# Conditioning sums spread over more stages of a two-layer diffusion step, and eight weight splits moved to VectorE

## The chip, the cores and the metric

The kernel runs on one core of a Trainium2 chip. The metric is the device time of one execution in microseconds (us), as the median of several runs. The engines are TensorE (PE in the profile, PEld its weight loads), VectorE (DVE), ScalarE (ACT), GpSimd (POOL) and SyncE (SP), whose queue issues most of the DMAs.

## The reference

One inference step of a network with two layers, in fp32. 1024 latent tokens and 128 context tokens, each 1024 wide, go through both layers. Layer 0 mixes tokens with a recurrent block, layer 1 with latent attention; each is followed by an MLP with a squared ReLU. Every sub-layer is normalized and then shifted, scaled and gated by vectors that come from a conditioning vector:

```python
def adaln_params(cond, w_ada, b_ada):
    mod = jax.nn.silu(cond) @ w_ada + b_ada
    return jnp.split(mod, 6, axis=-1)

def sq_relu_mlp(h, w1, w2):
    a = jax.nn.relu(h @ w1)
    return (a * a) @ w2

# per layer l, for the context (cond = c_ctx) and for the latents (cond = c):
sh1, sc1, g1, sh2, sc2, g2 = adaln_params(cond, ada_w[l], ada_b[l])
h = modulate(rms_norm(x, norm_mix[l]), sh1, sc1)
...   # recurrent block or attention, its projection first
x = x + g1[:, None, :] * out
h = modulate(rms_norm(x, norm_mlp[l]), sh2, sc2)
x = x + g2[:, None, :] * sq_relu_mlp(h, mlp_w1[l], mlp_w2[l])
```

## The kernel before

All activations stand transposed (features on the partitions) in three chunks of 384 tokens. Each matrix product is made of three fp32r matmuls (`mm3`, lines 145, 148 and 149): both operands are split into a high part and a rest, `hi` by a cast on ACT (line 163) and `lo` by a subtraction (line 164) on the engine that the caller names, VectorE or GpSimd. Weights stream through SBUF as pieces of 128 x 1024: a piece is loaded into one of two buffers `raw` (line 111), split into a pair `whi`, `wlo` of a small rotating set (`wslot`), and used. A `raw` buffer is free when its split is done.

The order of the work is written out by the program, engine by engine; a scheduler of the framework then moves instructions on each queue by its own estimate of the times, except where `keep_in_program_order` holds them.

**Conditioning sums.** Of the twelve vectors of both layers, seven (56 groups of 128 features) are computed with dot products: `ada` loads 128 rows of the transposed `ada_w` into a buffer (`raw` too, or one of its own in the second matrix; line 178) and `ada_dot` multiplies them on VectorE by the condition and accumulates, once for each of two conditions (line 169; the first half writes to `junk`, the second over the rows). I call a load and its two halves a sum. The 56 sums are a list that is taken off in order. Eight are taken in layer 0's output projection; 24 in the 16 passes over its first MLP matrix (one and two in turn); 24 in the second matrix, one whenever a weight buffer of the kind `g` is taken. Layer 1's MLP runs the same code with the list empty.

**The MLP** (`mlp`, called for both layers). The first matrix is multiplied in 16 passes, each with products of sums and differences of the operands (a scheme that needs seven products for eight). A pass takes two weight rows: `prep` loads them and splits them in three parts, `R0` and `R1` (on GpSimd in layer 0, on VectorE in layer 1) and, after four subtractions of raw weights on VectorE (line 454, `raw<-raw`), `TY` and `TX` on VectorE. Results are stored to DRAM as nine hidden tiles for each of eight groups (line 417 and its kin; four of a pass from SP). For the remaining rows there are four groups of plain products (`filler`), two ahead of the passes and two behind. While the last two run, the hidden tiles (`hid`, line 563) and the residual (`X`, line 579) are loaded back for the second matrix. That runs in 16 steps: GpSimd makes the differences of weights (line 599) and splits them, VectorE splits the hidden tiles and adds the results to the residual with the gate (line 334).

**Behind the MLP of layer 0** comes the attention's projection (`mla`): per chunk, VectorE computes the factor of the norm (`rstd`, lines 267 to 281), PE spreads it over partitions (line 288), VectorE and ACT write the normalized chunk (lines 315 and 320), and PE multiplies it with the weights of the first four output groups, then of three more.

Of the kernel before, what the change touches and what calls it, by code (L numbers as in the profile page):

```python
# [50 lines left out]
RG_STREAM = list(dict.fromkeys((_k, _n // 2 * 2 if _k == "g" else _n) for _k, _n, *_ in RG_ORDER))  # L51
# [14 lines left out]
class Emit:  # L66
    def __init__(self, nc, tc, ins, outs):
        self.nc, self.tc, self.I, self.O = nc, tc, ins, outs
        self.piece_i = 0
        self.opened = []  # L70
        self.pending = []
        self.wpx = None
        self.pin = False
        self.cap = 1 << 30
        self.upx = self.gx = None
        self.wcycle, self.wi = ["wp"], 0
        self.ready = []
        self.used, self.oldest = set(), 0
        self.ada_i = 0
        self.ada_jobs = []  # L80
        self.ada_quota = 0.0
        self.ada_rate = 0.0
# [12 lines left out]
    def prefetch(self, upto):  # L95
        nc = self.nc
        if self.wpx is None:
            upto = min(upto, len(RG_STREAM) + 3)
        while self.piece_i < min(upto, self.cap, len(STREAM)):
            raw = self.raw(STREAM[self.piece_i])  # L100
            eng = nc.vector if self.piece_i < len(RG_STREAM) else nc.gpsimd
            self.ready.append(self.wsplit(raw, eng))
            self.piece_i += 1
            self.ada_quota += self.ada_rate
            n = int(self.ada_quota)
            self.ada_quota -= n
            self.ada(n)
# [6 lines left out]
    def wslot(self):  # L114

        kind = self.wcycle[self.wi % len(self.wcycle)]
        self.wi += 1
        if kind == "g":
            self.ada(1, self.gx)
        pool, n = {"wp": (self.wp, 3), "x": (self.wpx, 1), "u": (self.upx, 1), "g": (self.gx, 4)}[kind]  # L120
        return tuple(pool.tile([128, 1024], F32R, tag=t, name=t, bufs=n) for t in ("whi", "wlo"))

# [48 lines left out]
                op0=ALU.mult, op1=ALU.mult, accum_out=self.mod[:, l, j, cond, k:k + 1],  # L171
            )

    def ada(self, n, room=None):
        for l, j, k in self.ada_jobs[:n]:
            w = (room or self.wp).tile([128, 1024], F32, tag="ada" if room else "raw", name="raw", bufs=1 if room else 2)
            n0 = (j * 8 + k) * 128
            self.nc.sync.dma_start(w, self.I["ada_wt"][l, n0:n0 + 128])
            self.ada_dot(w, l, j, k, 0, 1)
            if k == 7:  # L180
                self.mod_finish(l, j)
        del self.ada_jobs[:n]
# [226 lines left out]
    def mlp(self, p0, base, l, H, after_acc, after):  # L409
        nc = self.nc  # L410
# [26 lines left out]
        def filler(i0, n, f=None):  # L437
            if f:
                bring2.append(f)
            for i in range(i0, i0 + n, 4):  # L440
                self.group([(plain[i + j], p0 + i + j, range(8)) for j in range(4)], rhs, drain2, chunks=[2])
# [15 lines left out]
        def prep(p, part):  # L457
            if p == 16:
                if part:
                    self.cap = p0 + 8 + part  # L460
                    self.prefetch(self.cap)
                return
            m = 4 * (p // 2) + p % 2
            if part == 0:
                r = [self.raw(up_row(i), *((self.upx, 4) if p else ())) for i in (m, m + 2)]
                W[p] = {"r": r, "R0": self.wsplit(r[0], leng)}
                return
            w = W[p]
            r0, r1 = w["r"]
            a, b = slice(0, 512), slice(512, 1024)  # L470
            if part == 1:
                w["R1"] = self.wsplit(r1[:, b], leng, 512)
                add(r0[:, a], r1[:, a], r0[:, a], ALU.subtract)
                add(r1[:, a], r1[:, b], r1[:, a], ALU.subtract)
                add(r1[:, b], r1[:, b], r0[:, a], ALU.subtract)
                add(r0[:, b], r0[:, b], r1[:, b], ALU.subtract)
            else:
                w["TY"] = self.wsplit(r1, nc.vector)
                w["TX"] = self.wsplit(r0, nc.vector)

        self.wcycle, self.wi = ["wp", "wp", "wp", "x", "u"], 0
        for i in range(3):
            prep(0, i)
        tail = None
        for p in range(16):
            m = 4 * (p // 2) + p % 2
            w = W.pop(p)
# [55 lines left out]
                add(e, h12, d, ALU.subtract)  # L543
                put(m, 7, e, nc.sync)

            self.ada(1 + p % 2)
        tail()
        self.cap = p0 + 16
        self.release(self.upx)
# [31 lines left out]
            load((2, 4, 5, 6, 7, 8, 9, 9)[i], True)  # L581

        filler(8, 8, bring)
        load(12)

        self.release(self.gpool)
# [23 lines left out]
        for d in range(16):  # L610
# [3 lines left out]
            for i in range(2):  # L614
                n = 2 * d + i
                m = 2 * (n % 4)
# [451 lines left out]
    def mla(self):  # L1068
        nc, tc, I, O = self.nc, self.tc, self.I, self.O
# [7 lines left out]
        def drain(m, c, ps):  # L1077
            nc.scalar.copy(out=raw[c][:, m], in_=ps)
            if m < 4:
                self.sq_acc(stq[c], raw[c][:, m], m)  # L1080
            elif m < 6:
                self.sq_acc(stk[c], raw[c][:, m], m)

        def rq(c):
            yield 2.9
# [41 lines left out]

        rhs = lambda k, c: (H[c][0][:, k], H[c][1][:, k])
        self.dense(pi, range(4), rhs, drain, rq)
        self.release(self.xp, self.cbp)  # L1130
        keep = self.alloc(name="keep", bufs=1, side="right", reuse_waits="tile")
        ckv = [keep.tile([128, 2, NK], F32R, name=f"ckv{i}") for i in range(2)]
# [431 lines left out]
```

## Time and profile before

| | |
|---|---|
| median of 3 runs | 2857.14 us (2857.11 to 2859.36) |
| the profiled execution | 2860.27 us, span 2858.2 us, mean granted clock of TensorE 0.973 |
| first MLP matrix of layer 0, 16 passes | from 534 to 843 us of the span |
| second MLP matrix of layer 0 | from 896 to 1319 us |
| attention's projection, first half | from 1326 us |
| first MLP matrix of layer 1, 16 passes | from 2104 to 2398 us |
| second MLP matrix of layer 1 | from 2447 to 2836 us |

A row of the profile names the line, the engine, the operation and the tiles (`out<-in`), then how often, and its busy time and mean duration; idle time stands with what ended it, as in `[5.02 <-POOL wlo L164]`: idle for 5.02 us until GpSimd's instruction of line 164 on `wlo` was done. A stretch `A:B` is in us from the span's start.

### The profile page before, as it was taken

To read this page: it belongs to the slowest core of one execution; us is meant where nothing else is said; L and a number is where in the kernel's file an instruction comes from. 1 tells how busy PE (TensorE), PEld (TensorE's weight loads), DVE (VectorE), ACT (ScalarE), POOL (GpSimd) and SP (SyncE) were. 2 spreads that over 40 slices of the span, in tenths; PEclk is the share of its full clock that TensorE was granted. 3 is DMA by queue.
4 is the path that set the end of the run, shared out by engine and by line. 5 is a ranking of instruction groups with operands and counts; after the bars stand their busy time and mean duration, and the time that the engine had idled before them with its cause. 6 is when DMAs were issued, how large, how long until landed. Compare 5 with 4: busy or idle time off the path is not lost.

```text
span 2858.2 us, 40872 instructions
## 1 busy us (share of the span) xinstructions
PE 2663.3 (93%) x15355; PEld 2566.0 (90%) x15355; DVE 1945.2 (68%) x3445; ACT 1384.3 (48%) x2446; POOL 893.0 (31%) x560
## 2 busy tenths in 40 slices
PE   5999999999997989998997999998999999899997
PEld 2878899999996878998997999998999999799997
DVE  6788877896545999677465767762675554477777
ACT  4577834545443223334324878871465555333332
POOL 1000023212225877773242000001300002777774
PEclk9999999999998999999998999999999999999998
DMA  6122244474446444334135111116344345433332
GB/s 253 45 81 83 87 156 142 162 229 162 144 130 247 159 145 162 111 111 140 52 110 166 62 47 52 48 52 208 116 151 142 130 145 188 149 122 118 122 123 106
DMA packets 145718, 368.67 MB, mean 129 GB/s; under 512 B 15472, under 2 KB 77744, under 8 KB 143088
## 3 DMA queue, kind: packets, MB, share of 16 engines
q1 hardware_dynamic: 121712, 331.44, 34.6%
q10 hardware_dynamic: 23040, 31.47, 3.1%
q0 software_dynamic: 768, 3.15, 0.4%
q8 instruction: 121, 1.98, 0.3%
q14 instruction: 77, 0.63, 0.1%
HBM read 268.83 MB, written 94.54 MB: 127 GB/s over the span
## 4 chain that ended last, share of the span: by engine, by line
PE 41%; DVE 5%; DMA 3%; POOL 2%; issue 2%; ACT 2%; SPq 0%; DVEq 0%; ACTq 0%; POOLq 0%
PE ps L145 9%; PE ps L148 9%; PE ps L149 9%; PE ps L1317 2%; DMA raw<-wts 2%; POOL wlo L164 1%; PE ps L1261 1%; PE ps L1264 1%; PE ps L1265 1%; PE ps L1262 1%; PE ps L1263 1%; PE ps L1343 1%; PE ps L1342 1%; PE ps L1341 1%; POOL raw L599 1%
## 5 line engine op out<-in xcount | busy, mean ns | idle before, releaser
L164 POOL TENSOR_TENSOR wlo<-raw,whi 128x1024 fp32r<-128x1024 f32 x233 | 569.8, 2453 | 1662.5 <-ACT whi L163 1399.2
L163 ACT CAST whi<-raw 128x1024 fp32r<-128x1024 f32 (+1 forms) x349 | 347.6, 1008 | 671.7 <-POOL raw L599 269.1
L145 PE MATMUL ps<-hhi,whi 128*128 128x384 f32 x1576 | 533.0, 342 | 22.0 <-ACT hhi L319 10.3
L148 PE MATMUL ps<-hlo,whi 128*128 128x384 f32 x1576 | 536.4, 340 | 13.7 <-DVE hlo L320 13.4
L149 PE MATMUL ps<-hhi,wlo 128*128 128x384 f32 x1576 | 532.6, 340 | 8.2 <-POOL wlo L164 7.9
L145 PE MATMUL ps<-hid,whi 128*128 128x384 f32 x1408 | 480.0, 344 | 51.3 <-DVE X L334 33.5
L334 DVE SCALAR_TENSOR_TENSOR X<-ps,mod,X 128x384 f32<-128x384 f32 (+2 forms) x768 | 379.4, 534 | 204.8 <-PE ps L149 171.0
L148 PE MATMUL ps<-hid,whi 128*128 128x384 f32 x1408 | 477.8, 339 | 0.0
L149 PE MATMUL ps<-hid,wlo 128*128 128x384 f32 x1408 | 462.9, 339 | 2.5 <-POOL wlo L164 2.5
L145 PEld LDWEIGHTS ps<-hid,whi 128*128 128x128 f32 x1408 | 269.0, 191 | 67.1 <-DVE X L334 39.1
L145 PEld LDWEIGHTS ps<-hhi,whi 128*128 128x128 f32 x1576 | 300.3, 191 | 32.2 <-ACT hhi L319 11.5
L148 PEld LDWEIGHTS ps<-hlo,whi 128*128 128x128 f32 x1576 | 300.9, 191 | 17.1 <-DVE hlo L320 17.0
L149 PEld LDWEIGHTS ps<-hhi,wlo 128*128 128x128 f32 x1576 | 300.6, 191 | 11.7 <-POOL wlo L164 10.0
L164 DVE TENSOR_TENSOR hid<-hid 128x768 fp32r<-128x768 f32 x144 | 208.1, 1465 | 92.5 <-ACT hid L163 92.5
L149 PEld LDWEIGHTS ps<-hid,wlo 128*128 128x128 f32 x1408 | 267.1, 190 | 3.3 <-POOL wlo L164 3.3
L148 PEld LDWEIGHTS ps<-hid,whi 128*128 128x128 f32 x1408 | 269.8, 192 | 0.0
L599 POOL TENSOR_TENSOR raw<-raw 128x256 f32<-128x256 f32 x256 | 252.8, 990 | 17.9
L164 DVE TENSOR_TENSOR wlo<-raw,whi 128x1024 fp32r<-128x1024 f32 x116 | 136.4, 1186 | 128.3 <-ACT whi L163 127.5
L163 ACT CAST hid<-hid 128x768 fp32r<-128x768 f32 x144 | 117.4, 834 | 157.4 <-DMA hid<-hid 143.8
L1266 DVE TENSOR_REDUCE mx<-ps 128x1 f32<-128x384 f32 (+1 forms) x200 | 108.6, 543 | 76.5 <-PE ps L1265 75.0
L148 PE MATMUL ps<-S,whi 128*128 128x384 f32 x384 | 130.4, 340 | 6.1 <-DVE S L164 6.1
L149 PE MATMUL ps<-S,wlo 128*128 128x384 f32 x384 | 130.4, 340 | 1.6 <-DVE wlo L164 1.5
(213 smaller groups left out, 5194.5 us busy)
## 6 DMA issues: line engine op xcount, KB each, us to landing
raw<-wts SPq DMA_DIRECT2D x221, 512.0 KB, 3.8
hid<-hid SPq DMA_DIRECT2D x144, 384.0 KB, 4.7
raw<-ada_wt SPq DMA_DIRECT2D x56, 512.0 KB, 3.8
hid<-st ACTq DMA_DIRECT2D x128, 192.0 KB, 2.0
hid<-st SPq DMA_DIRECT2D x128, 192.0 KB, 1.9
adaw<-ada_n SPq DMA_DIRECT2D x24, 512.0 KB, 4.3
xs<-X SPq DMA_DIRECT2D x6, 1536.0 KB, 5.4
X<-xs SPq DMA_DIRECT2D x12, 768.0 KB, 9.5
```

What stands on the lines that cost most here:

```text
L145: mm = nc.tensor.matmul(ps, lhsT=w[0], rhs=h[0], start=first, stop=False, **kw)
L148: nc.tensor.matmul(ps, lhsT=w[0], rhs=h[1], start=False, stop=False, **kw)
L149: nc.tensor.matmul(ps, lhsT=w[1], rhs=h[0], start=False, stop=last, **kw)
L163: nc.scalar.copy(out=hi, in_=src)
L164: (lo_eng or nc.vector).tensor_tensor(out=lo, in0=src, in1=hi.bitcast(F32), op=ALU.subtract)
L334: self.nc.vector.scalar_tensor_tensor(out=self.X[c][:, m, a:b], in0=ps[:, a:b], scalar=self.mod[:, l, j, cond, m:m + 1], in1=self.X[c][:, ...
L599: sub = lambda out, x, y: nc.gpsimd.tensor_tensor(out=out, in0=x, in1=y, op=ALU.subtract)
L1261: nc.tensor.matmul(ps, lhsT=qh, rhs=kh[:, a:b], start=True, stop=False)
L1262: nc.tensor.matmul(ps, lhsT=qh, rhs=kl[:, a:b], start=False, stop=False)
L1263: nc.tensor.matmul(ps, lhsT=ql, rhs=kh[:, a:b], start=False, stop=False)
L1266: nc.vector.tensor_reduce(out=mx[:, j:j + 1], in_=ps, axis=AX.X, op=ALU.max)
L1317: nc.tensor.transpose(ps[:, j * 128:(j + 1) * 128], p[:, (t * 3 + j) * 128:(t * 3 + j + 1) * 128], self.ident)
```

## The change

Three things. (1) In the first matrix two sums are taken in each pass from the third on (28 for 24), with their loads held in program order. (2) In the second matrix only every third buffer of the kind `g` takes a sum (12 for 24), and the last eight are taken in the attention's projection, at the drains of three of its first four groups. (3) From the last pass over the first matrix to the end of the plain groups behind it, the pieces of weights (eight in each layer) are split by VectorE and not by GpSimd.

```diff
@@ class Emit: __init__, prefetch
+        self.on_dve = False
...
-            eng = nc.vector if self.piece_i < len(RG_STREAM) else nc.gpsimd
+            eng = nc.vector if self.piece_i < len(RG_STREAM) or self.on_dve else nc.gpsimd
             self.ready.append(self.wsplit(raw, eng))
@@ wslot
         if kind == "g":
-            self.ada(1, self.gx)
+            if self.ada_i % 3 == 0:
+                self.ada(1, self.gx)
+            self.ada_i += 1
@@ ada
-    def ada(self, n, room=None):
+    def ada(self, n, room=None, pin=False):
...
-            self.nc.sync.dma_start(w, self.I["ada_wt"][l, n0:n0 + 128])
+            ld = self.nc.sync.dma_start(w, self.I["ada_wt"][l, n0:n0 + 128])
+            if pin:
+                self.tc.keep_in_program_order(ld)
@@ mlp: prep
             if p == 16:
                 if part:
+                    self.on_dve = True
                     self.cap = p0 + 8 + part
                     self.prefetch(self.cap)
@@ mlp: the loop over 16 passes, and behind it
-            self.ada(1 + p % 2)
+            if p > 1:
+                self.ada(2, pin=True)
...
         filler(8, 8, bring)
+        self.on_dve = False
         load(12)
@@ mla: drain, and behind the first four groups
+            if 0 < m < 4:
+                self.ada(1)
...
         self.dense(pi, range(4), rhs, drain, rq)
+        self.ada(len(self.ada_jobs))
         self.release(self.xp, self.cbp)
```

Lines of the new kernel stand a few numbers further on (169 becomes 172, 454 becomes 459, 178 becomes 181).

First place: VectorE in a steady pass over layer 0's first matrix. `st` are results of the pass, `raw` the weights that are subtracted, `wlo` the splits that the next pass needs. Before:

```order
L454 TENSOR_TENSOR st<-st 128x384 x3
L454 TENSOR_TENSOR raw<-raw 128x512
L454 TENSOR_TENSOR st<-st 128x384
L454 TENSOR_TENSOR st<-ps,cell 128x384
L454 TENSOR_TENSOR raw<-raw 128x512 x2
L454 TENSOR_TENSOR st<-ps,cell 128x384
L454 TENSOR_TENSOR raw<-raw 128x512
L454 TENSOR_TENSOR st<-ps,cell 128x384
L164 TENSOR_TENSOR wlo<-raw,whi 128x1024 x2
```

The same place in the new kernel:

```order
L459 TENSOR_TENSOR st<-st 128x384
L459 TENSOR_TENSOR st<-ps,cell 128x384
L459 TENSOR_TENSOR raw<-raw 128x512
L172 SCALAR_TENSOR_TENSOR junk,mod<-raw,cb 128x1024
L172 SCALAR_TENSOR_TENSOR raw,mod<-raw,cb 128x1024
L172 SCALAR_TENSOR_TENSOR junk,mod<-raw,cb 128x1024
L172 SCALAR_TENSOR_TENSOR raw,mod<-raw,cb 128x1024
L459 TENSOR_TENSOR raw<-raw 128x512
L459 TENSOR_TENSOR st<-ps,cell 128x384
L459 TENSOR_TENSOR raw<-raw 128x512
L459 TENSOR_TENSOR st<-ps,cell 128x384
L167 TENSOR_TENSOR wlo<-raw,whi 128x1024 x2
```

The four halves of two sums now stand between the second and the third subtraction of raw weights.

Second place: SP's queue in layer 0's second matrix. `hid_2` to `hid_4` are the hidden groups that are loaded ahead, `wts` weights, `ada_wt` the rows of a sum. Before:

```order
L111 DMA raw<-wts 128x1024
L178 DMA raw<-ada_wt 128x1024
L563 DMA hid<-hid_2 128x768 x3
L563 DMA hid<-hid_3 128x768 x3
L111 DMA raw<-wts 128x1024
L178 DMA raw<-ada_wt 128x1024
L111 DMA raw<-wts 128x1024
L178 DMA raw<-ada_wt 128x1024 x2
L111 DMA raw<-wts 128x1024
L563 DMA hid<-hid_3 128x768 x2
```

In the new kernel, from the twelfth sum's load on:

```order
L181 DMA raw<-ada_wt 128x1024
L570 DMA hid<-hid_2 128x768 x2
L112 DMA raw<-wts 128x1024
L570 DMA hid<-hid_2 128x768 x2
L112 DMA raw<-wts 128x1024
L570 DMA hid<-hid_2 128x768 x3
L570 DMA hid<-hid_3 128x768 x3
L112 DMA raw<-wts 128x1024 x3
L570 DMA hid<-hid_3 128x768 x2
```

All twelve loads stand ahead of the first row of this piece or in it; behind it the queue holds hidden tiles and weights alone.

Third place: VectorE where layer 0's MLP ends and the attention's projection begins. `X<-ps` are the last residuals of the third chunk, `cell` and `hlo` the first chunk's normalization, `sv` opens the second chunk's factor. Before:

```order
L252 TENSOR_TENSOR acc<-acc,cell 128x384
L334 SCALAR_TENSOR_TENSOR X<-ps,mod,X 128x256
L334 SCALAR_TENSOR_TENSOR X<-ps,mod,X 128x128
L315 SCALAR_TENSOR_TENSOR cell<-X,mod,ps 128x384
L320 SCALAR_TENSOR_TENSOR hlo<-cell,mod,hhi 128x384
L315 SCALAR_TENSOR_TENSOR cell<-X,mod,ps 128x384
L267 TENSOR_SCALAR sv<-ps 128x3
```

The same place in the new kernel:

```order
L172 SCALAR_TENSOR_TENSOR raw,mod<-raw,cb 128x1024
L257 TENSOR_TENSOR acc<-acc,cell 128x384
L339 SCALAR_TENSOR_TENSOR X<-ps,mod,X 128x256
L339 SCALAR_TENSOR_TENSOR X<-ps,mod,X 128x128
L320 SCALAR_TENSOR_TENSOR cell<-X,mod,ps 128x384
L172 SCALAR_TENSOR_TENSOR junk,mod<-raw,cb 128x1024
L325 SCALAR_TENSOR_TENSOR hlo<-cell,mod,hhi 128x384
L172 SCALAR_TENSOR_TENSOR raw,mod<-raw,cb 128x1024
L172 SCALAR_TENSOR_TENSOR junk,mod<-raw,cb 128x1024
L320 SCALAR_TENSOR_TENSOR cell<-X,mod,ps 128x384
L272 TENSOR_SCALAR sv<-ps 128x3
```

The halves of the sums now stand among the residuals, the normalization and the factor; six sums are through before the last row of the second chunk's factor.

## Prediction, made before the changed kernel ran

> **What bounds the kernel now.** I read the page first: TensorE (PE) is busy 93% of the span, so time can only come from the stretches in which PE waits or crawls.
>
> ```profile
> span 2858.2 us, 40872 instructions
> PE 2663.3 (93%) x15355; PEld 2566.0 (90%) x15355; DVE 1945.2 (68%) x3445; ACT 1384.3 (48%) x2446; POOL 893.0 (31%) x560
> ```
>
> The trace holds its own control for those stretches. The same MLP code runs twice, and the conditioning sums exist in layer 0 alone. I cut both passes at equal matmul counts. In the busy time by stretch, the number after PE's busy time counts matmuls, and DVE (VectorE) is the third engine. First come six stretches of layer 0 (crowded passes of the first matrix, its other passes, the last plain groups, then the second matrix in three parts), then the same six of layer 1.
>
> ```profile
> core 0: us, PE busy (x) PEld busy (x) DVE busy (x) ACT busy (x) POOL busy (x), PEclk, DMA share, GB/s
> 531.70:653.50 121.80, 111.08 (x601) 108.54 (x601) 117.00 (x167) 54.12 (x93) 26.62 (x12) 0.96 0.67 215
> 653.50:837.20 183.70, 183.70 (x1052) 183.44 (x1052) 95.04 (x129) 93.77 (x169) 33.22 (x18) 1.00 0.41 138
> 837.20:896.30 59.10, 45.76 (x239) 43.19 (x237) 19.69 (x28) 30.05 (x46) 19.02 (x8) 0.91 0.85 308
> 896.30:1008.80 112.50, 97.08 (x500) 93.01 (x501) 100.25 (x139) 29.09 (x32) 99.67 (x60) 0.91 0.44 141
> 1008.80:1138.70 129.90, 112.79 (x601) 107.46 (x601) 121.93 (x180) 36.77 (x40) 94.33 (x59) 0.96 0.46 156
> 1138.70:1317.30 178.60, 176.38 (x1013) 174.84 (x1013) 130.36 (x205) 62.40 (x78) 129.35 (x85) 1.00 0.39 128
> 2101.80:2209.20 107.40, 105.47 (x601) 104.59 (x600) 64.69 (x89) 58.48 (x98) 0.00 (x0) 1.00 0.45 154
> 2209.20:2392.70 183.50, 183.50 (x1053) 183.50 (x1052) 97.12 (x143) 93.79 (x165) 0.00 (x0) 1.00 0.39 131
> 2392.70:2446.90 54.20, 44.95 (x240) 43.17 (x238) 21.24 (x18) 29.85 (x46) 19.16 (x8) 0.94 0.83 307
> 2446.90:2548.30 101.40, 92.89 (x500) 90.78 (x501) 55.63 (x91) 30.11 (x32) 81.27 (x61) 0.95 0.31 99
> 2548.30:2654.00 105.70, 104.99 (x602) 104.09 (x601) 78.31 (x123) 36.45 (x42) 79.19 (x55) 1.00 0.39 132
> 2654.00:2834.00 180.00, 177.43 (x1017) 175.05 (x1016) 137.05 (x223) 58.19 (x74) 126.52 (x86) 1.00 0.31 103
> ```
>
> Layer 0 loses 121.8 - 107.4 = 14.4 us in the crowded passes, where DVE is busy 117.0 of 121.8, and 11.1 and 24.2 us in the first two parts of the second matrix, where DVE is busy 89% and 94%. Where DVE has room the layers agree within 1.4 us. The waits (520 to 660, then 1000 to 1100) name the same engine:
>
> ```profile
> PE ps L145 <- DVE st L454: 4.6, 3, 2.2
> PE ps L145 <- DVE X L334: 16.3, 13, 3.9
> ```
>
> The next rows say when the sums of layer 0 are loaded (520 to 645, 890 to 1010, 1005 to 1125; the last two share one), and what the two halves of a sum cost on DVE in 520 to 860 and in 895 to 1125.
>
> ```profile
> L178 SPq DMA_DIRECT2D raw<-ada_wt x22: 327/328/818, 526.3 to 639.0; - x22
> L178 SPq DMA_DIRECT2D raw<-ada_wt x13: 327/328/333, 890.8 to 1005.5; - x13
> L178 SPq DMA_DIRECT2D raw<-ada_wt x12: 327/330/333, 1005.5 to 1114.5; - x12
> L169 DVE SCALAR_TENSOR_TENSOR junk<-raw,cb 128x1024 bf16<-128x1024 f32 x24 | 33.9, 1413 | 4.9 <-DMA raw<-ada_wt 4.7
> L169 DVE SCALAR_TENSOR_TENSOR raw<-raw,cb 128x1024 f32<-128x1024 f32 x24 | 33.4, 1391 | 0.1
> L169 DVE SCALAR_TENSOR_TENSOR junk<-raw,cb 128x1024 bf16<-128x1024 f32 x24 | 47.3, 1971 | 16.2 <-DMA raw<-ada_wt 16.1
> L169 DVE SCALAR_TENSOR_TENSOR raw<-raw,cb 128x1024 f32<-128x1024 f32 x24 | 40.0, 1667 | 0.2
> ```
>
> So 22 sums crowd into seven passes, and the second matrix carries 24, twelve to about 1000 and twelve after. A sum holds DVE for about 2.8 us in the first matrix (two halves), and in the second for (47.3 + 40.0 + 16.2) / 24 = 4.3 us with its wait for the load.
>
> **The change, part by part.** *First matrix: the 22 early sums and two late ones become 28, two in each pass from the third on.* In the new order the four halves of a steady pass stand just ahead of a subtraction of raw weights (`raw<-raw`). DVE idles there now, because that subtraction waits for GpSimd (POOL):
>
> ```profile
> 708.76 0.69 DVE L454 TENSOR_TENSOR raw<-raw 128x512 f32<-128x512 f32 x1 [5.02 <-POOL wlo L164]
> 712.02 2.36 DVE L164 TENSOR_TENSOR wlo<-raw,whi 128x1024 fp32r<-128x1024 f32 x2 [0.36 <-ACT whi L163]
> 717.46 2.98 DVE L454 TENSOR_TENSOR st<-st 128x384 f32<-128x384 f32 x3 [3.08 <-ACT st L420]
> ```
>
> Two sums at 2.8 us are 5.6 us in a gap of 5.02; the 0.6 us over goes into the 3.08 us of idle time behind the splits, so PE should not see them. Their loads are pinned on SP's queue ahead of the four stores of a pass, which wait for DVE, so they land early; behind a late one would wait these stores and the next pass's weights. I take 12.4 of the 14.4 us as gained and leave 2 us for the third and fourth pass, where four halves stand ahead of a split. Ends: 14.4 us gained, and, at today's 14.4 / 22 = 0.65 us for each of 28 sums, 3.9 us lost.
>
> *Last plain groups, both layers: eight splits of weights go from POOL to DVE.* In 820 to 920 PE waits for these weights, and SP's next load for POOL (838 to 925):
>
> ```profile
> PE ps L145 <- ACT whi L163: 11.8, 5, 5.5
> SPq L111 <- POOL wlo L164: 19.4, 6, 5.3
> 860.00:880.00 20.00, 18.21 (x101) 17.12 (x99) 6.68 (x6) 11.36 (x17) 8.69 (x4) 1.00 1.02 406
> 883.17 3.64 SPq L111 DMA_DIRECT2D raw<-wts  x2
> ```
>
> The page has a split on either engine:
>
> ```profile
> L164 POOL TENSOR_TENSOR wlo<-raw,whi 128x1024 fp32r<-128x1024 f32 x233 | 569.8, 2453 | 1662.5 <-ACT whi L163 1399.2
> L164 DVE TENSOR_TENSOR wlo<-raw,whi 128x1024 fp32r<-128x1024 f32 x116 | 136.4, 1186 | 128.3 <-ACT whi L163 127.5
> ```
>
> A split takes 2453 ns on POOL and 1186 ns on DVE, so a buffer comes free 1.3 us sooner, and in this stretch DVE is busy 19.69 of 59.1 us. But the second matrix needs its first weights, which SP issues at 883.17, behind loads that fill the DMA (share 1.02). PE would finish the groups sooner and then wait for that load. I take 3 us in layer 0, for a burst that begins about 3 us sooner, and 1 us in layer 1, whose first weights come at the same place. Ends: at 1052 matmuls in 183.7 us, 239 matmuls need 41.7 us, so 17.4 and 12.3 us could go at most; 3 us could be lost in each, if the splits on DVE wait behind hidden tiles still in flight.
>
> *Second matrix: 24 sums become 12.* The diff spaces them over every third buffer, but the new order still places all twelve loads before the tiles of the fourth hidden group, as densely as now. So the first part keeps its 11.1 us, and the second, with no sum left, becomes layer 1's: 24 us gained. Ends: 11.1 + 24.2 = 35.3 us at most; 17.6 us if each sum costs alike.
>
> *Attention's projection: eight sums come in.* Here DVE normalizes the first chunk (L315, L320) while PE waits for each part, and in the same queue computes the second chunk's factor (to 1339.49):
>
> ```profile
> 1320.00:1340.00 20.00, 14.38 (x68) 14.17 (x69) 16.13 (x41) 8.34 (x14) 4.68 (x3) 0.74 0.36 127
> 1324.83 0.60 DVE L315 SCALAR_TENSOR_TENSOR cell<-X,mod,ps 128x384 f32<-128x384 f32 x1
> 1329.21 0.16 DVE L267 TENSOR_SCALAR sv<-ps 128x3 f32<-128x3 f32 x1 [1.83 <-PE ps L260]
> 1339.33 0.16 DVE L281 SCALAR_TENSOR_TENSOR sy<-st,sy 128x3 f32<-128x3 f32 x1
> 1343.95 1.66 DVE L315 SCALAR_TENSOR_TENSOR cell<-X,mod,ps 128x384 f32<-128x384 f32 x3 [4.45 <-PE ps L288]
> 1379.45 0.16 DVE L267 TENSOR_SCALAR sv<-ps 128x3 f32<-128x3 f32 x1 [10.66 <-PE ps L260]
> ```
>
> The new order puts six sums ahead of that factor, a seventh into the second chunk's normalization and the eighth into the idle 10.66 us, where it costs nothing. Behind their loads on SP stand a store of a chunk and weights that PE needs only in the projection's second half. Six at 2.8 us are 16.8; DVE's idle 4.45 us ahead of the second chunk and the 1.83 us cover 6.3; the seventh adds 2.8. PE waits 13 us longer. The row nearest to a sum's price here is the first matrix's, since POOL is busy 4.68 of 20 us, as little as there (26.62 of 121.8). Ends: 10 us if the seventh is covered too; seven at 4.3 us less 4.45, or 26 us, if they run as in the second matrix.
>
> POOL's share bears on that price. The Trainium skill ("SBUF — State Buffer", Who interferes with whom) says that a VectorE instruction with two SBUF inputs and a GpSimd instruction that reads SBUF exclude each other: the later one waits. The trace agrees: the halves take 1971 and 1667 ns where POOL works most of the time. By that rule alone all 4.68 us of POOL's work would come on top, and the loss here would be 17.7 us; the sum would be -22.7 us and the runs' time 2834. My sum keeps to the rows.
>
> **The sum.** -12.4 - 3 - 1 - 24 + 13 = -27.4 us. The profiled execution took 2860.3 us around its span of 2858.2, 3.1 over the median of the runs, 2857.1. So the trace gives 2832.9, and the runs **2830 us**, 1.0% faster.
>
> **The rivals.** The first rests on how long a sum's load takes in the first 2000 us:
>
> ```profile
> DMA to landing us min/median/max: 3.4/3.8/12.5
> ```
>
> - *Slower: the projection's sums wait for their loads.* Their buffers are two, shared with the weights, and a store of a whole chunk stands between the third and fourth load on SP. If each load took the longest of these, 12.5 us, two buffers would give one sum per (12.5 + 2.8) / 2 = 7.65 us; seven cost 53.6 less 4.45 = 49, against 40.4 us gained elsewhere: 2857 + 9 = 2866. It decides from 6.4 us a sum on. Against it: the DMA share there is 0.36, and the median is 3.8 us.
> - *Pacing does not help the first matrix:* PE loses 0.65 us for each of 28 sums. Then +3.9 stands for -12.4: 2846. For it, GpSimd's split, which the idle DVE waits for, reads SBUF as the sums do; against it, 3.08 us of idle time behind.
> - *The plain groups lose their whole excess:* -17.4 - 12.3 stands for -4: 2804; half of that 2817. For it, SP's 19.4 us of waits for POOL; against it, the full DMA.
> - *Each sum of the second matrix costs alike:* -17.6 for -24: 2836. The split 11.1 to 24.2 speaks against it.
>
> **How the numbers follow.** Forecast 0.65, inside 2820 to 2841; first matrix 0.10; plain groups 0.10; alike 0.10; slower 0.05. The likeliest gives 2830. The range 2814 to 2847 takes in the projection's end at 26 us (2843), the rival on the first matrix and half of the one on the plain groups; the rest of that one and the slower case stay out. A measurement here tells 0.2%, or 5.7 us, from no change. All cases but one end below 2851; since several prices could miss together I give 0.92 for faster, 0.04 for the same and 0.04 for slower.
>
> **What would show it.** Right: the crowded passes' 601 matmuls take about 109 us; the second matrix's first 500 still take about 112 and the next 601 about 106; the attention's projection has longer waits for DVE, 13 us in all. Wrong: PE waits for `st L454` in every pass; DVE in the projection waits for `raw<-ada_wt`; or the last plain groups run without a wait and the second matrix starts at once.

## The result and the profile after

The changed kernel takes 2834.9 us (median of four runs, 2834.3 to 2835.6) where the kernel before, timed beside it, takes 2858.2: a ratio of 0.9914, 95% interval 0.9902 to 0.9927. It is faster by 0.9%. The forecast was 2830 in a range of 2814 to 2847. The profiled execution took 2835.1 us, 1.9 around its span, so the traces differ by 25.0 us where the prediction's sum was 27.4. One execution each of experiments 2 and 9 was slow throughout (4918 and 3818 us, granted clock 0.85 and 0.64) and stands in no figure below.

The page of the changed kernel begins so:

```profile
span 2833.2 us, 40867 instructions
PE 2656.6 (94%) x15355; PEld 2561.3 (90%) x15355; DVE 1951.3 (69%) x3461; ACT 1385.0 (49%) x2446; POOL 840.8 (30%) x544
```

The matmuls are the same 15355 and VectorE (DVE) is busy for about as long as before. PE is idle for 176.6 us where it was idle for 194.9: 18.3 of the 25.0 us came out of its waits, and the other 6.7 out of its busy time. The busy time of the changed kernel follows, cut at the same matmul counts as the first six stretches of the prediction: crowded passes of the first matrix, its other passes, the last plain groups, and the second matrix in three parts.

```profile
core 0: us, PE busy (x) PEld busy (x) DVE busy (x) ACT busy (x) POOL busy (x), PEclk, DMA share, GB/s
533.20:642.50 109.30, 106.08 (x601) 104.46 (x601) 85.62 (x112) 55.37 (x96) 23.86 (x12) 1.00 0.55 190
642.50:826.80 184.30, 184.30 (x1053) 183.51 (x1052) 141.71 (x202) 92.31 (x166) 34.13 (x18) 1.00 0.52 183
826.80:887.60 60.80, 44.22 (x240) 42.58 (x239) 28.61 (x34) 30.04 (x46) 0.26 (x1) 0.89 0.82 297
887.60:1003.10 115.50, 99.91 (x501) 95.62 (x501) 100.86 (x147) 29.81 (x32) 100.49 (x61) 0.88 0.43 138
1003.10:1108.10 105.00, 104.54 (x601) 104.10 (x601) 78.09 (x121) 36.38 (x41) 78.79 (x55) 1.00 0.40 133
1108.10:1286.30 178.20, 176.69 (x1014) 174.90 (x1013) 133.75 (x205) 60.80 (x77) 132.30 (x88) 1.00 0.39 129
```

Two stretches fell, 121.8 to 109.3 and 129.9 to 105.0 us, and two did not: the last plain groups (59.1 to 60.8) and the second matrix's first part (112.5 to 115.5). In the other passes of the first matrix DVE's busy time rose from 95.0 to 141.7 us, and PE did not lose a microsecond of its 184.3.

All kernels below were cut in the same way: the next table holds, in us, the time between the starts of the first and the last matmul of a stage. "Second matrix" is given in its first 500, next 601 and remaining matmuls; its excess is its whole time less that of layer 1's second matrix in the same trace, where no sum stands. One stage of one trace scatters: layer 0's last plain groups are 52.5 to 55.6 us in the seven kernels that leave them as the change has them. The ratio of the runs is to the kernel before, timed beside it, with its interval.

| kernel (sums in the first matrix, second matrix, projection) | first matrix | last plain groups | second matrix | excess | projection | plain groups, layer 1 | span | ratio |
|---|---|---|---|---|---|---|---|---|
| before (24, 24, 0) | 308.4 | 53.6 | 112.5 + 130.1 + 180.4 | 33.9 | 111.0 | 48.5 | 2858.2 | 1 |
| the change (28, 12, 8) | 296.4 | 55.1 | 115.8 + 105.2 + 179.9 | 13.6 | 120.7 | 47.8 | 2833.2 | 0.9914 (0.9902-0.9927) |
| first matrix only (28, 20, 0) | 297.2 | 52.8 | 117.1 + 118.4 + 179.9 | 27.3 | 110.5 | 49.5 | 2839.8 | 0.9936 (0.9923-0.9948) |
| loads not pinned (28, 12, 8) | 310.0 | 54.7 | 111.5 + 111.0 + 179.9 | 15.9 | 120.9 | 47.8 | 2847.4 | 0.9963 (0.9950-0.9977) |
| second matrix pinned (28, 12, 8) | 296.2 | 54.6 | 105.9 + 110.0 + 187.6 | 16.4 | 120.1 | 47.9 | 2833.4 | 0.9915 (0.9902-0.9929) |
| second matrix pinned (28, 20, 0) | 297.5 | 53.9 | 108.5 + 119.4 + 186.3 | 25.3 | 111.0 | 48.8 | 2839.4 | 0.9934 (0.9921-0.9948) |
| three sums a pass (36, 12, 0) | 309.2 | 52.5 | 116.0 + 105.3 + 180.8 | 15.8 | 111.3 | 47.7 | 2833.5 | 0.9925 (0.9912-0.9939) |
| all in the first matrix (48, 0, 0) | 317.3 | 54.3 | 99.1 + 107.1 + 180.0 | -2.2 | 110.7 | 47.4 | 2826.6 | 0.9899 (0.9885-0.9913) |
| splits on POOL (28, 12, 8) | 296.9 | 53.4 | 115.0 + 105.2 + 180.6 | 10.8 | 120.5 | 48.8 | 2834.0 | 0.9918 (0.9905-0.9932) |
| stores on POOL's queue (28, 12, 8) | 297.6 | 51.5 | 112.1 + 109.2 + 179.7 | 13.3 | 120.4 | 46.4 | 2830.4 | 0.9912 (0.9898-0.9925) |
| half of the residual's loads (28, 12, 8) | 297.2 | 52.7 | 118.3 + 105.2 + 180.2 | 15.4 | 120.5 | 43.7 | 2829.8 | 0.9885 (0.9870-0.9901) |
| eight sums in layer 1 (28, 12, 0) | 297.7 | 55.6 | 117.9 + 105.2 + 179.8 | 15.8 | 111.6 | 47.3 | 2827.4 | 0.9884 (0.9871-0.9898) |
| the same, stores on POOL's queue | 297.9 | 50.6 | 113.0 + 110.3 + 180.0 | 15.1 | 110.9 | 47.7 | 2829.6 | 0.9874 (0.9859-0.9890) |
| the same, and splits on POOL | 297.4 | 52.0 | 116.1 + 105.2 + 180.6 | 13.5 | 110.9 | 48.2 | 2829.9 | 0.9888 (0.9870-0.9905) |

Two waits of PE show where DVE let go of it. Among PE's waits in the changed kernel, over the first matrix (535 to 832) and then over the second (887 to 1290), these lines stand (total, times, longest):

```profile
PE ps L148 <- DVE st L459: 2.2, 3, 1.0
...
PE ps L148 <- DVE X L339: 12.9, 9, 2.9
```

and in the kernel before, over the second matrix (885 to 1320; L334 is the later L339):

```profile
PE ps L145 <- DVE X L334: 28.6, 22, 3.9
```

The first matrix's wait for `st`, 4.6 us in the crowded passes before, is 2.2 us over all sixteen. That is a part of the gain there: over the 601 crowded matmuls all of PE's idle time fell from 10.7 to 3.2 us, and its busy time from 111.1 to 106.1 us, with a granted clock of 1.00 for 0.96. The second matrix's wait for `X` fell by 15.7 us, to less than half.

A new stall stands in the last plain groups. The changed kernel in order of time (start, duration, engine and operation, in brackets the idle time before it and what ended it):

```profile
857.99 0.33 PE L148 MATMUL ps<-hhi,whi 128*128 128x384 f32 x1
...
860.76 0.32 SPq L586 DMA_DIRECT2D X<-xs  x1
...
862.09 0.33 ACTq L422 DMA_DIRECT2D hid<-acc  x1
862.47 0.49 ACT L428 ACTIVATE acc<-ps 128x384 f32<-128x384 f32 x1 [4.55 <-DMA raw<-wts]
862.99 0.52 ACT L425 ACTIVATE acc<-acc 128x384 f32<-128x384 f32 x1
...
871.44 0.33 ACTq L422 DMA_DIRECT2D hid<-acc  x1
871.81 0.83 ACT L166 CAST hid<-hid 128x768 fp32r<-128x768 f32 x1 [8.30 <-DMA X<-xs]
872.55 1.04 ACT L166 CAST whi<-raw 128x1024 fp32r<-128x1024 f32 x1
...
873.64 0.69 PE L148 MATMUL ps<-hhi,whi 128*128 128x384 f32 x1 [12.88 <-ACT whi L166]
```

ScalarE (ACT) computes nothing between 863.5 and 871.8. Its next entry is the issue of its own store (`ACTq L422`), which stands until 871.44, and a load of the residual (`X<-xs`) ends that wait. Behind it in ACT's queue stands the cast of the weights for which PE then waits 12.88 us, though these weights had landed at 862.0. The trace says why the store waited for a load: both signal their end on the same semaphore (105 in the trace). The load, issued at 860.76, landed on it at 871.37, and the store, which was to use it next, was held until then.

### The profile page after: what moved, and what is told of

The parts are those of the page before. It is cut to its first block, busy times and chain, and to the rows that moved or that the text cites. A ratio compares the mean times of both kernels' runs of the same rounds, so it can differ in the third digit from the quotient of the medians.

```text
span 2833.2 us, 40867 instructions
## 1 busy us (share of the span) xinstructions
PE 2656.6 (94%) x15355; PEld 2561.3 (90%) x15355; DVE 1951.3 (69%) x3461; ACT 1385.0 (49%) x2446; POOL 840.8 (30%) x544
## 5 line engine op out<-in xcount | busy, mean ns | idle before, releaser
L167 POOL TENSOR_TENSOR wlo<-raw,whi 128x1024 fp32r<-128x1024 f32 x217 | 526.5, 2436 | 1680.8 <-ACT whi L166 1066.1
L151 PE MATMUL ps<-hlo,whi 128*128 128x384 f32 x1576 | 535.3, 340 | 16.3 <-DVE hlo L325 16.1
L339 DVE SCALAR_TENSOR_TENSOR X<-ps,mod,X 128x384 f32<-128x384 f32 (+2 forms) x768 | 380.4, 534 | 218.7 <-PE ps L152 186.2
L167 DVE TENSOR_TENSOR wlo<-raw,whi 128x1024 fp32r<-128x1024 f32 (+1 forms) x132 | 151.6, 1158 | 164.8 <-ACT whi L166 163.8
L607 POOL TENSOR_TENSOR raw<-raw 128x256 f32<-128x256 f32 x256 | 244.4, 958 | 17.6
L166 ACT CAST hid<-hid 128x768 fp32r<-128x768 f32 x144 | 117.1, 834 | 138.1 <-DMA hid<-hid 119.1
## 6 DMA issues: line engine op xcount, KB each, us to landing
X<-xs SPq DMA_DIRECT2D x12, 768.0 KB, 10.7
```

The costliest lines, as they stand in the source:

```text
L151: nc.tensor.matmul(ps, lhsT=w[0], rhs=h[1], start=False, stop=False, **kw)
L166: nc.scalar.copy(out=hi, in_=src)
L167: (lo_eng or nc.vector).tensor_tensor(out=lo, in0=src, in1=hi.bitcast(F32), op=ALU.subtract)
L339: self.nc.vector.scalar_tensor_tensor(out=self.X[c][:, m, a:b], in0=ps[:, a:b], scalar=self.mod[:, l, j, cond, m:m + 1], in1=self.X[c][:, ...
L607: sub = lambda out, x, y: nc.gpsimd.tensor_tensor(out=out, in0=x, in1=y, op=ALU.subtract)
```

## The experiments

**1. The first matrix alone.** The kernel before, with one edit in the passes and the pin that it needs:

```
-            self.ada(1 + p % 2)
+            if p > 1:
+                self.ada(2, pin=True)
```

> The kernel before with the spacing of the first matrix alone: two pinned sums in each pass from the third on (28), the other 20 at the second matrix's weight buffers as before, none in the attention's projection, splits on POOL. Theory: the first matrix gains its 12 us by itself; the second matrix has four sums fewer, which gives 6 us if each sum there costs alike (35.3 / 24 = 1.5 us) and 8 us if only the later sums cost (24.2 / 12 = 2.0 us each): 2857 - 12 - 6 to 8 = 2837 to 2839 us. Rival (the 12 us of the first matrix came from elsewhere in the change, spacing alone does not help): 2849 to 2861 us.

Measured 2842.0 us, ratio 0.9936; the time lies 3 us over the expected range, as the kernel before stood at 2860.8 beside it. The first matrix takes 297.2 us, 11.2 less than before, so its gain is its own. The second matrix, with 20 sums, gains 7.6 us (415.4 against 423.0): its middle part gains 11.7 (118.4 against 130.1), and its first part loses 4.6.

**2. The same counts without the pin.** The change, with `self.ada(2)` for `self.ada(2, pin=True)`; in the order that results, 26 of the 28 sums stand close together again.

> The change with the same numbers of sums, two in each pass from the third on, but their loads not pinned, so that the scheduler may set them earlier: 26 of the 28 then stand close together in the first passes again. Theory (the first matrix gains by the even spacing, which the pin makes): the matrix loses its 12 us and, at 14.4 us for 22 crowded sums, 3 us more for the 26: first matrix 308 to 311 us instead of 296, 2847 to 2850 us. Rival (the later start and the count per pass do it, not the pin): 296 us, 2835 us.

Measured 2848.6 us, ratio 0.9963; first matrix 310.0 us, 13.6 more than with the pin. The gain of the first matrix comes from the even spacing, and the pin is what makes the spacing. The rival falls.

**3. The second matrix spaced in earnest.** The prediction had found that the change's twelve sums there still crowd at its start. This edit keeps each at its place in the program:

```
-                self.ada(1, self.gx)
+                self.ada(1, self.gx, pin=True)
```

> The change, with the loads of the twelve sums of the second matrix pinned to their place in the program, so that they stand at every third weight buffer through the whole matrix and not all at its beginning. Theory (forecast's ground for the second matrix: sums cost where they crowd): the first 500 matmuls of the second matrix took about 116 us in the change against 99.5 in layer 1, which has no sums; most of these 16.5 us go and the sums that move to the last part find VectorE idle 45 of 176 us there: 2820 to 2826 us. Rival (each sum of the second matrix costs alike wherever it stands, 22 us over 12 sums gone, so 1.5 to 1.8 us each): unchanged, 2833 to 2837 us. Second rival (a pinned load holds SP's queue and the weights behind it): slower, 2840 us.

Measured 2835.2 us, ratio 0.9915: no change. The busy time of this kernel in the second matrix's three parts, and PE's longest group of waits there:

```profile
887.40:993.30 105.90, 94.78 (x500) 91.97 (x501) 78.12 (x112) 30.12 (x32) 86.71 (x61) 0.92 0.34 112
993.30:1103.30 110.00, 106.21 (x602) 104.06 (x602) 88.86 (x132) 37.77 (x42) 87.04 (x58) 1.00 0.45 149
1103.30:1290.90 187.60, 180.97 (x1024) 178.12 (x1023) 148.82 (x241) 61.51 (x77) 131.93 (x86) 0.99 0.40 135
```

```profile
PE ps L148 <- DVE X L339: 14.0, 14, 2.6
```

The first part gained 9.9 us and the other two lost 12.5. PE waits for DVE's residuals as long as with crowded sums (14.0 against 12.9), in more and shorter waits (14 against 9). DVE has room on average, 148.8 busy of 187.6 us in the last part, and a sum still costs PE time. My theory falls here, and the prediction's rival "each sum costs alike" holds. The second rival, pinned loads that hold up the weights, asked for 2840 us and falls too.

**4. All 48 sums in the first matrix.** Three a pass in passes 2 to 9, four from 10 on, none later:

```
-                self.ada(2, pin=True)
+                self.ada(3 + (p > 9), pin=True)
...
-            if 0 < m < 4:
-                self.ada(1)
```

> The change with all 48 sums in the first matrix: three pinned in each of the passes 2 to 9, four in 10 to 15; none in the second matrix or the projection. With four sums VectorE's work is 14.3 + 2 x 2.9 = 20.1 us in a pass of 18.9, so VectorE bounds six passes: 7 us lost or more. Theory (each sum in the second matrix costs PE 1.1 to 1.4 us wherever it stands, 13 to 17 us over twelve; the projection's eight cost 9.7): 2835 - 13 - 9.7 + 7 = 2819 us. Rival 1 (what makes the second matrix of layer 0 slower than layer 1's is not its sums): 2832 us. Rival 2 (full passes make PE wait for all that stands behind the sums, half a sum each): 8 x 1.45 in the passes with three and 6 x 4 in those with four, 2830 us or more.

Measured 2830.0 us, ratio 0.9899. Its busy time in the first matrix (two stretches) and in the first two parts of the second:

```profile
530.10:641.10 111.00, 106.81 (x601) 104.45 (x601) 93.49 (x126) 55.24 (x96) 24.89 (x12) 1.00 0.63 206
641.10:844.60 203.50, 189.08 (x1053) 184.60 (x1052) 181.40 (x266) 93.94 (x166) 39.61 (x19) 0.99 0.62 202
...
904.70:1003.30 98.60, 91.95 (x500) 89.56 (x500) 58.73 (x92) 30.45 (x32) 81.43 (x61) 0.95 0.32 102
1003.30:1110.20 106.90, 105.28 (x601) 104.06 (x601) 77.94 (x122) 36.53 (x41) 79.19 (x55) 1.00 0.40 130
```

Without sums the second matrix of layer 0 is as fast as layer 1's (an excess of -2.2 us), so rival 1 falls: its whole excess is the sums. Taking -2.2 as the zero, a sum there costs (33.9 + 2.2) / 24 = 1.5 us in the kernel before, (27.3 + 2.2) / 20 = 1.5 in experiment 1, 18.6 / 12 = 1.6 when pinned, and 15.8 / 12 = 1.3 in the change. The first matrix paid 20.9 us for its twenty further sums, between the 7 of the theory and the 36 of the second rival; so the time came out at 2830 and not at 2819.

**5. 36 sums in the first matrix.** As in the change, but three a pass from pass 8 on, and none in the projection:

> The change with its eight late sums moved from the attention's projection into the first matrix: two pinned sums in the passes 2 to 7, three in 8 to 15 (36), twelve in the second matrix as in the change, none in the projection. In the change's trace a steady pass takes 18.9 us and VectorE is busy 134.6 of 177.2 us, 14.3 us a pass; a third sum of 2.9 us makes 17.2. Theory: the first matrix still hides them and the projection gives back the 9.7 us that it grew by: 2824 to 2827 us. Rival (a sum costs PE 0.65 us in the first matrix once VectorE is nearly full): 8 x 0.65 = 5 us of that are lost again, 2830 us. Second rival (the projection's 9.7 us did not come from its sums): 2835 us or more.

Measured 2837.8 us, ratio 0.9925. The projection gave back 9.4 us (111.3), so that loss was its sums'. The first matrix lost 12.8, which is 1.6 us for each of the eight. The rival's kind was right, and its price of 0.65 too low. The kernel's busy time over the later passes, and its wait in the first matrix:

```profile
645.00:843.00 198.00, 190.14 (x1069) 187.49 (x1068) 159.00 (x230) 96.33 (x171) 38.50 (x18) 0.99 0.56 189
```

```profile
PE ps L148 <- DVE st L459: 10.1, 7, 3.4
```

DVE is busy 159 of 198 us, far from full, and PE waits for it all the same: two sums a pass fit the gaps of the queue, a third does not.

**6. The projection's eight sums in the second matrix.** Experiment 3 with `% 3 < 2` for `% 3 == 0`, and no sum in the projection:

> The change with the projection's eight sums moved into the second matrix: 20 there, pinned to two of every three weight buffers, none in the projection. Theory (a sum of the second matrix costs PE about 1.4 us wherever it stands, as (403.5 - 387.0) / 12 in the kernel with its twelve sums pinned): second matrix 387 + 28 = 415 us, 14 more than in the change, less 9.7 for the projection: 2839 us. Rival (sums that are spaced cost nothing in the second matrix, and what the pinned kernel lost is the pinning itself): 403.5 us again and 9.7 gained, 2828 us.

Measured 2840.2 us, ratio 0.9934. The second matrix took 414.2 us and the projection 111.0. The second matrix took 10.7 us more than with its twelve pinned sums (403.5), or 1.3 us for each of the eight, so spaced sums are not free there and the rival falls. In the projection the eight cost 9.7 us, 1.2 each. That they cost more in the second matrix isn't shown: the intervals of this kernel and of experiment 3 overlap.

**7. Splits back on POOL.** The change without its third part:

```
-            eng = nc.vector if self.piece_i < len(RG_STREAM) or self.on_dve else nc.gpsimd
+            eng = nc.vector if self.piece_i < len(RG_STREAM) else nc.gpsimd
```

> The change without its third part: the eight splits of weights in the last plain groups of both layers stay on POOL, the sums are spaced as in the change. In the change's trace the last plain groups took 1.5 us longer than before in layer 0 and 0.7 us shorter in layer 1, and the second matrix of layer 1 1.7 us shorter. Theory (the splits' gain was given back by a new wait of ACT): about the same as the change, 2834 to 2838 us. Rival 1 (the splits earn the 4 us of the forecast and something else cost the plain groups as much): 2839 us. Rival 2 (the splits on VectorE harm, in the plain groups and in the second matrix's first part, which lost 3.5 us): 2830 us.

Measured 2837.1 us, ratio 0.9918 against 0.9914: no difference that these runs can tell. In layer 1 the plain groups take 47.8 us with the splits on DVE and 48.8 here, which is the forecast's 1 us. One pair can't show so little, since traces with the splits on DVE and the rest of these groups as in the change read 47.3 to 48.8; but their mean is 47.8, and that of the three with the splits on POOL (the kernel before, experiments 1 and 7: 48.5 to 49.5) is 48.9. In layer 0 nothing is saved (55.1 against 53.4).

**8. The store off ACT's queue.** In the second set of plain groups:

```
-            put(m, 5, t)
+            put(m, 5, t, nc.gpsimd if bring2 else nc.scalar)
```

> The change, with the stores of hidden tiles in the last plain groups issued from POOL's queue where ACT's issued them; nothing else differs. Theory: ACT's cast of the weights waited 8.3 us behind its own store, which waited for a DMA semaphore that a load of the residual held, and PE waited 12.9 us for that cast; without the store ahead of it the groups lose 8 to 12 us: 2823 to 2827 us. Rival (the DMA share of 1.0 bounds the stretch, and the cast is late because its weights land late): within 2 us of the change, 2833 to 2837 us.

Measured 2835.1 us, ratio 0.9912: the same as the change. This kernel's waits over the last plain groups, of PE and of ACT:

```profile
PE ps L148 <- ACT whi L166: 14.5, 3, 8.4
...
ACT whi L166 <- DMA raw<-wts: 12.7, 5, 5.3
ACT hid L166 <- DMA hid<-hid: 11.7, 6, 2.6
```

ACT no longer waits for its store (8.3 us in the change). It waits for the loads of the weights, and PE's longest wait fell only from 12.9 to 8.4 us. The groups gained 3.6 us and the second matrix's first part 3.7, of which the middle part gave 4.0 back. So the store was a real cause of the 12.9 us, and it was not the bound: with it gone, PE still waits 14.5 us for weights there, where it waited 18.8.

**9. Half of the residual's loads.** In both layers POOL's zeros stand for half of the residual:

```
-                    nc.sync.dma_start(self.X[c][:, k:k + 4], self.xs_d[l][c, :, k:k + 4])
+                    nc.sync.dma_start(self.X[c][:, k:k + 2], self.xs_d[l][c, :, k:k + 2])
```

> The change, with half of each load of the residual left out in both layers (two of four blocks of 128 rows loaded, the others filled with zeros by POOL): that half of the computation is not done, all the rest is the same. Six loads of 786 KB become 393 KB, at the 415 GB/s of the stretch 5.7 us of transfers fewer. Theory (the full DMA bounds the last plain groups, of which ACT's wait for its store is one form): layer 0's last plain groups 55.1 -> 48 to 51 us and layer 1's 47.8 -> 43 to 45, 2825 to 2830 us. Rival (an engine's queue and not the DMA bounds them): both within 1 us, 2835 us.

The kernel leaves out half of the residual, so only its time counts. Measured 2829.5 us, ratio 0.9885. In layer 1 the plain groups fell from 47.8 to 43.7 us, as a bound by the transfers asks. PE's wait there in the change, and then in this kernel:

```profile
PE ps L148 <- ACT whi L166: 11.9, 1, 11.9
```

```profile
PE ps L148 <- ACT whi L166: 7.8, 1, 7.8
```

In layer 0 they fell to 52.7 us, 2.4 less, which is inside their scatter, and the second matrix's first part grew by as much. A wait behind ACT's own store would shrink with the loads too, but it isn't what holds layer 1: in experiment 8, with no store on ACT's queue, PE's longest wait there is still 10.5 us. So the transfers are shown as the bound for layer 1; for layer 0 this run leaves it open.

**10. Eight sums in layer 1's first matrix.** The gate of layer 1's MLP is needed only in that layer's second matrix. Its eight sums leave layer 0; the condition vectors are loaded again after the attention:

```
+        cb4 = self.cond("cb4", side="right")
...
-                self.ada(2, pin=True)
+                self.ada(1 if l else 2, pin=True)
...
-            if 0 < m < 4:
-                self.ada(1)
```

> The change with its eight late sums moved out of layer 0: the condition vectors are loaded again after the attention, and one pinned sum stands in each of eight passes of layer 1's first matrix; nothing is left in the attention's projection. Theory (two sums a pass cost PE nothing where VectorE idles, and the projection's 9.7 us came from its sums): 2835 - 9.7 = 2825 us, layer 1's first matrix still 293 to 294 us. Rival (sums cost PE 1.2 us each wherever they stand): 2834 us, layer 1's first matrix 303 us.

Measured 2829.0 us, ratio 0.9884 (0.9871 to 0.9898), under the change's 0.9914 with no overlap of the intervals. The projection takes 111.6 us. Layer 1's first matrix in the change, and then with the sums:

```profile
2082.20:2375.80 293.60, 291.89 (x1668) 291.02 (x1667) 161.58 (x233) 153.68 (x266) 0.00 (x0) 1.00 0.41 137
```

```profile
2077.60:2370.70 293.10, 291.43 (x1669) 291.14 (x1668) 180.24 (x267) 153.41 (x266) 0.00 (x0) 1.00 0.46 155
```

DVE works 18.7 us more and PE loses nothing: one sum a pass is free there. The median lies 4 us over the theory's 2825; of that, 2.6 us is the kernel before standing higher beside this kernel than beside the change; by the ratios the kernel is 0.3% faster than the change.

**11 and 12. The same with the stores on POOL's queue, and then with the splits on POOL again.**

> The same as the kernel with the late sums in layer 1's first matrix, and besides it the hidden tiles of the last plain groups stored from POOL's queue. In the kernel that differed from the change in this store alone, PE's longest wait in the last plain groups fell from 12.9 to 8.4 us, the groups from 55.1 to 51.5 and the second matrix's first part from 115.8 to 112.1, the second part grew by 4.0, and the runs did not differ. Theory (the store's wait is real, the full DMA gives most of it back): 2 to 4 us under the kernel without this edit, 2821 to 2823 us. Rival (all of it is given back): the same, 2825 us.

> The same as the kernel with the late sums in layer 1's first matrix and the stores on POOL's queue, but with the eight splits of the last plain groups on POOL again. Theory (the transfers bound the last plain groups, so the engine of the splits does not matter): within 2 us of the kernel with the splits on VectorE. Rival (the splits earn the forecast's 4 us once no store holds ACT): 4 us slower than that kernel, 2 to 3 of them in layer 0's last plain groups.

Measured 2823.8 us (2820.8 to 2831.4) and 2831.7 us (2822.6 to 2834.3), ratios 0.9874 and 0.9888. Their intervals overlap with each other and with experiment 10. The one with the stores moved has the lowest median and beats the change; that the stores or the splits add to what experiment 10 gave isn't shown. The trace of experiment 11, in the table, is of the slowest of its four executions (2831.4 us). In the trace of experiment 12 layer 1's first matrix takes 296.8 us for experiment 10's 293.1; the 3.7 us lie in its first 100 matmuls, and behind these the two run alike, so the sums are free there too. In the traces the splits on DVE save 1.4 us in layer 0's plain groups and 0.5 in layer 1's, and the three parts of the second matrix take 403.3 us with them and 401.9 without. The runs of experiment 12 lie on the side of its rival, 7.9 us slower by the medians and 4 by the ratios; since the intervals overlap, the rival is left open.

## Why the prediction was right, point by point

**First matrix, -12.4: right.** Measured -12.0. The crowded 601 matmuls take 109.3 us, where about 109 was forecast. Its ground, gaps of DVE that hold two sums a pass, is shown by experiments 1 and 2 and limited by experiment 5: the gaps hold two sums and not three.

**Last plain groups, -3 and -1: wrong in layer 0, right in layer 1.** Measured +1.5 and -0.7. The +1.5 lies inside layer 0's scatter, but a gain of 3 us would be 50.6, and none of the seven traces lies below 52.5. The step that failed is "a burst that begins about 3 us sooner". The first load of the residual on SP's queue, in the kernel before and then in the changed one:

```profile
861.93 0.42 SPq L579 DMA_DIRECT2D X<-xs  x1
```

```profile
849.91 0.41 SPq L586 DMA_DIRECT2D X<-xs  x1
```

The first matrix's last matmul starts at 842.7 and 832.2, so the loads begin 1.5 us sooner after it (17.7 against 19.2), and the stall behind ACT's store takes more than that away: with the store moved, the groups take 51.5 us in experiment 8 and 50.6 in experiment 11. In the traces of experiments 7 and 12 the splits' engine is worth -1.7 and +1.4 us in layer 0, nothing that the scatter lets one see; experiment 8 that the store caused 4.5 us of the longest wait. In layer 1 the -0.7 agrees with the means of experiment 7, -1.1. The rival that the groups lose their whole excess fell with the measured +1.5.

**Second matrix, -24: the size about right, the reason half wrong.** Measured -22.0. Where the time would go was as forecast: the first part keeps its loss (115.5 us against the forecast's 112), and the middle becomes layer 1's (105.0 against 106). What failed is the reason under "the first part keeps its 11.1 us, and the second, with no sum left, becomes layer 1's: 24 us gained": it takes the 24 us for the price of the sums that go, and so a sum for dearer in one part than in the other. Halving the sums gained what twelve sums cost, (36.1 - 15.8) = 20.3 us beside the 1.7 by which layer 1's matrix shrank as well. The rival "each sum of the second matrix costs alike" is what the runs show, at 1.3 to 1.6 us a sum over four arrangements. Its own number, -17.6, missed by 4.4 us where my -24 missed by 2.0 on the other side, so that my number came nearer was luck. Its price, 35.3 / 24 = 1.5, is the one that experiment 4 finds for the kernel before; the change's twelve sums cost only 1.3 each, and layer 1's matrix shrank besides.

**Attention's projection, +13: right in kind, mis-sized.** Measured +9.7, a little under the end of 10. PE's waits there, after and then before:

```profile
PE ps L148 <- ACT hhi L324: 7.9, 1, 7.9
PE ps L151 <- DVE hlo L325: 3.7, 5, 1.5
PE ps L293 <- DVE sy L286: 3.0, 3, 1.3
```

```profile
PE ps L145 <- ACT hhi L319: 5.0, 1, 5.0
PE ps L288 <- DVE sy L281: 1.5, 2, 1.1
PE ps L148 <- DVE hlo L320: 0.6, 1, 0.6
```

They grew by 2.9, 3.1 and 1.5 us, 7.5 of the 9.7; the rest is PE's busy time for the same 609 matmuls, 106.1 us for 103.9. The mis-sized term is the idle time of DVE that was to cover 6.3 us. In the changed kernel the second chunk's normalization begins so:

```profile
1320.25 1.66 DVE L320 SCALAR_TENSOR_TENSOR cell<-X,mod,ps 128x384 f32<-128x384 f32 x3 [0.70 <-PE ps L293]
```

It starts 32.1 us behind the second matrix's last matmul (1288.2), where it started 24.8 us behind it before (1343.95 and 1319.2). So the six sums ahead of it, 16.3 us at the measured 2.7, cost 7.3, and 9 us of them were covered. The other 2.4 us of the loss are what the seventh sum takes there. The sums did not wait for loads, which answers the slower rival, and their halves were as short as in the first matrix:

```profile
L172 DVE SCALAR_TENSOR_TENSOR junk<-raw,cb 128x1024 bf16<-128x1024 f32 x7 | 10.1, 1443 | 0.0
L172 DVE SCALAR_TENSOR_TENSOR raw<-raw,cb 128x1024 f32<-128x1024 f32 x7 | 8.9, 1270 | 0.0
```

Against these, the twelve of the second matrix, beside a busy POOL:

```profile
L172 DVE SCALAR_TENSOR_TENSOR raw<-raw,cb 128x1024 f32<-128x1024 f32 x12 | 24.2, 2019 | 0.2
L172 DVE SCALAR_TENSOR_TENSOR junk<-raw,cb 128x1024 bf16<-128x1024 f32 x12 | 21.1, 1756 | 13.8 <-DMA raw<-ada_wt 13.8
```

A sum takes 2.7 us of DVE in the projection and 3.8 in the second matrix. The Trainium skill ("SBUF — State Buffer", Who interferes with whom) has VectorE's two-input instructions and GpSimd's reads exclude each other; these two rows agree with it in direction. The time that the prediction worked out from that rule, 2834 us, is by chance the measured one: it came from a loss of 17.7 us in the projection, and the loss was 9.7.

**The sum.** The terms' errors are +0.4, +4.5 and +0.3, +2.0, and -3.3 us, 3.9 together. The layer-1 second matrix (-1.7) and the stretches with no change make up the rest to -25.0, against -27.4. The runs' median lies 4.9 us over the forecast. About half of that is the sum's; the other part is the 3.1 us that the prediction took off because the profiled execution before stood so far above its runs, which the changed kernel's does not (2835.1 against 2834.9). The total owes something to luck: the plain groups' error and the projection's have opposite signs.

## What to carry to other kernels

In this kernel VectorE's average load did not tell what a small VectorE job costs TensorE: two sums a pass were free at 77% load, where VectorE waited for another engine anyway, a third cost 1.6 us at 80%, and in the second matrix each cost about 1.5 us however they were spaced, at 79% too. That the price is set by what stands behind the job in the queue at that moment fits all of this and was not tested by itself. So look for the stage where the engine waits for others, fill its gaps with a pinned number per pass, and stop at the number that the gap holds; a result needed late may go to another layer's gap. Where the transfers are full, as in the last plain groups (DMA share 1.02), faster work ahead of them may only move the waits.

## What the runs showed of the hardware

Here an engine that issues its own store stood still while that store waited. ACT idled 8.30 us between two instructions with only the store's issue between them, until a load that SP's queue had issued landed on the semaphore that the store was to use; with the store on POOL's queue that wait was gone.

The stall went on costing after it ended. The matmul of 128x384 that took 0.33 us at 857.99 took 0.69 us at 873.64, right after PE's 12.88 us of idle time; most of those behind it took 0.52 us until 877.6, and 0.33 to 0.35 again from 877.84 on. The granted clock from 873 to 878 was 0.53, and 0.89 over the plain groups.
